# Attention: queries and keys turned by transposing DMA in 16-bit planes instead of on TensorE

## The chip, the cores and the metric

The kernel runs on one core of a Trainium2 chip. The metric is the device time of one execution in microseconds (us), the median of several runs. The engines are called as in the profile: PE is TensorE (PEld its weight loads), DVE is VectorE, ACT is ScalarE, POOL is GpSimd, SP is the engine that issues most transfers. A bank is one of the eight PSUM banks that PE writes, 128 x 512 f32 each.

## The reference

One encoder block over 512 tokens of width 2048, in f32: a combined input projection, two kinds of attention heads, an output projection, and a gated feed-forward block.

```python
h = rmsnorm(x, g_mix[layer])
proj = jnp.einsum('bsd,de->bse', h, w_in[layer])
qa, ka, va, qb, kb, vb = jnp.split(proj, offs, axis=-1)
...
out_a = rmsnorm(mixer_a(qa, ka, va, g_q_a[layer], g_k_a[layer]), g_out_a[layer])
out_b = rmsnorm(mixer_b(qb, kb, vb), g_out_b[layer])
x = x + jnp.einsum('bse,ed->bsd', concat(out_a, out_b), w_out[layer])
h2 = rmsnorm(x, g_ffn[layer])
gate, up = jnp.split(jnp.einsum('bsd,df->bsf', h2, w_gate_up[layer]), 2, axis=-1)
x = x + jnp.einsum('bsf,fd->bsd', jax.nn.silu(gate) * up, w_down[layer])
return rmsnorm(x, g_final)
```

The first kind ("A", `mixer_a`): eight query heads of 128 channels over two key/value heads, RMS-normalised queries and keys with an axial rotary, softmax over all 512 keys. The second kind ("B", `mixer_b`): eight heads with their own keys and values, a rotary on the first 32 channels of each head, and three windowed and dilated branches that are merged by their softmax denominators; the kernel does this as one softmax with an additive mask.

## The kernel before, in words

Every product is made of three matmuls on operands that are split into a high and a low part (`split`: ACT copies the high part, DVE subtracts it from the source for the low part; `mm3`, L228 to L230). The tokens are four row tiles of 128 (`NT`). What PE works on is cut into units: a unit loads a chunk of a weight (`raw`), splits it (`w` or `wide`, `wl`) and multiplies. Program order is written out by hand: each engine runs its instructions in the order in which the Python code issues them, and waits where an operand is not there yet.

Attention has no stage of its own. It is a list of tasks (`attention_tasks`), and `give` hands them out between the matmuls of the projection units: each step of a unit adds credit (`HEAD_RATE`, 2.8 in the first units and 1.3 later), each task costs some. The units beside it are the last chunks of the input projection (`in_plain`; their rows are scaled and evicted by ACT as `evqkB` and stored to DRAM), then chunks of the output projection.

A head is four slots, one for each row tile of its queries. `head_slot(s)` issues what is due in slot s: the score of this slot's head (three matmuls into a bank) and its exponential on ACT, the scaling by the denominator on DVE one slot later, the turn of a block of probabilities on PE five slots later (`pt`, L613, four transposes into one bank, then the split into `pTh` and `pTl`), and the product with the values six slots later (`pv`). Two tasks stand ahead of a head's first score. Four slots ahead, `tq` turns the head's queries: four PE transposes (L563), one for each row tile, into one bank, which is then split into `qTh` and `qTl`. Two slots ahead, `tk` does the same for the keys of a B head (L574); A heads take keys that were turned earlier (`kTA`).

The sources of these turns are `qA[0]` and `qA[1]` (four A heads' queries each, 128 x 512 for a row tile) and `qkB[0]` to `qkB[3]` (two B heads' queries and two B heads' keys each). `qA[1]` and all of `qkB` come back from DRAM by a transfer of 1 MB (`reload`); the rotary of a `qkB` is four DVE operations (`rope_partial`). All these tiles, the planes and words of the change among them, are slots of a shared pool in SBUF that are handed out in turn (`slot`).

The gate and up stage, which follows much later, has a pattern of the same kind: ACT copies a 128 x 512 f32 tile into two planes of 16 bits (L1255), SP issues a transposing transfer of eight 128 x 128 tiles of 16 bits (L1258), and ACT interleaves the planes again (L1264).

Of the kernel before, what the change touches and what calls it, by code (L numbers as in the profile page):

```python
# [14 lines left out]
U16 = mybir.dt.uint16  # L15
AF = mybir.ActivationFunctionType
# [4 lines left out]
P = 128  # L21
S = 512
D = 2048
HD = 128
NT = S // P
# [41 lines left out]
COLUMN_BLOCKS = 3  # L67
SUM_LEAD = 6
ATTEND_PAST = 4


def f32(ap):
# [4 lines left out]
def encoder_block(ctx, tc, x, w_in, g_q_a, g_k_a, w_out, w_gate_up, w_down, g_final, x_t, gains, c_ident, c_mask,  # L77
                  c_axial, c_partial, out):
    nc = tc.nc
# [13 lines left out]
    def slot(base, dtype=F32, shape=(P, 512)):  # L93
        return sp.tile(list(shape), dtype, tag="s", name=nm(base))
# [11 lines left out]
    def bank():  # L106
        return banks.popleft()

    def release(*tiles):
        banks.extend(tiles)  # L110
# [102 lines left out]
    def split(src, name, gain=None, at=None):  # L213
        if at is None:
            hi, lo = slot(name + "h", F32R), slot(name + "l", F32R)
        else:
            hi, lo = (place(*h) for h in at)
        if gain is None:
            nc.scalar.activation(hi, src, AF.Copy)  # L219
            nc.vector.tensor_tensor(lo, src, f32(hi), op=OP.subtract)  # L220
        else:
            nc.scalar.activation(hi, src, AF.Copy, scale=gain)
            nc.vector.scalar_tensor_tensor(lo, src, gain, f32(hi), op0=OP.mult, op1=OP.subtract)
        return hi, lo
# [307 lines left out]
    def rope_partial(q):  # L532
# [7 lines left out]
        nc.vector.tensor_tensor(rot, rot, ropeb[:, 0][:, :, None, :].to_broadcast([P, NT, 4, PARTIAL]), op=OP.mult)  # L540
        nc.vector.tensor_tensor(rot, rot, tmp, op=OP.add)

    oT = {}
    o_dram = {(g, h): dp.tile([P, 512], F32, tag=f"o{g}{h}", name=f"o{g}{h}")
              for g, n in SPILLED.items() for h in range(n)}
# [4 lines left out]
    class Head:  # L550
        def __init__(self, kind, h):
            self.kind, self.h = kind, h
            self.p, self.o = {}, None
            self.negm, self.z, self.rz = None, None, None

        def tq(self):
            ps = bank()
            for t in range(NT):
                if self.kind == "A":
                    src = qA[self.h // 4][t][:, (self.h % 4) * HD:(self.h % 4 + 1) * HD]  # L560
                else:
                    src = qkB[self.h // 2][t][:, (self.h % 2) * HD:(self.h % 2 + 1) * HD]
                nc.tensor.transpose(ps[:, t * P:(t + 1) * P], src, ident)  # L563
            self.q = split(ps, "qT", HD ** -0.5 if self.kind == "B" else None, at=self.home("q"))
            release(ps)

        def tk(self):
            if self.kind == "A":
                self.k = kTA[self.h // (NHA // NKV)]
                return  # L570
            ps = bank()
            for t in range(NT):
                lo = 256 + (self.h % 2) * HD
                nc.tensor.transpose(ps[:, t * P:(t + 1) * P], qkB[self.h // 2][t][:, lo:lo + HD], ident)  # L574
            self.k = split(ps, "kT", at=self.home("k"))
            release(ps)

        def home(self, part):
            return HEAD_HOMES[part][self.h % 2] if self.kind == "B" and self.h > 1 else None
# [79 lines left out]
    def head_slot(s):  # L659
        def at(lag, f, only=None):  # L660
            head, i = head_at(s - lag)
            if head and (only is None or i == only):
                f(head, i)
        at(VALUE_LAG + 1, lambda head, i: head.add_squares(), NT - 1)
        at(0, Head.score)
        at(1, Head.norm)
        at(TURN_LAG, Head.pt)
        at(0, Head.exp)
        at(VALUE_LAG, Head.pv)
        at(VALUE_LAG, lambda head, i: head.fin(), NT - 1)  # L670
        at(-4, lambda head, i: head.tq(), 0)
        at(-2, lambda head, i: head.tk(), 0)

    def weighed(cost, f):
        f.cost = cost
# [2 lines left out]
    def light(cost, tasks):  # L678
        return [weighed(cost, f) for f in tasks]

    def attention_tasks():
        def q_tasks(j):
            return norm_rope(lambda t: (qA[j][t], qA[j][t]), 4, "q")

        def both(cost, *lists):
            return [weighed(cost, lambda fs=fs: [f() for f in fs]) for fs in zip(*lists)]

        qA.update({j: {} for j in range(2)})
        qkB.update({j: {} for j in range(4)})
# [8 lines left out]
        todo += light(0.6, [lambda kv=kv: transpose_k_a(kv) for kv in range(NKV)]) + [heads[0].tq, heads[0].tk]  # L698
        todo += light(0.1, [lambda: reload("qA1", qA[1])])
        extra = {}  # L700

        def at(slot, tasks):
            extra.setdefault(slot, []).extend(tasks)
        at(20, light(0.1, [lambda: nc.sync.dma_start(mask, c_mask)]))
        q_squares, q_turned, q_scaled = q_tasks(1)
        for t in range(NT):
            at(t // 2, both(0.8, q_squares[t:t + 1]))
            at(2 + 2 * t, both(0.9, q_turned[t:t + 1]))
            at(3 + 2 * t, both(0.9, q_scaled[t:t + 1]))
        for j in range(4):  # L710
            s = NT * (NHA + 2 * j)
            at(s - 11, light(0.1, [lambda j=j: reload(f"qkB{j}", qkB[j])]))
            at(s - 7, light(0.9, [lambda j=j: rope_partial(qkB[j]["whole"])]))
        for h in range(NHB):
            s = NT * (NHA + h)
            at(s + 2, light(0.1, [lambda h=h: load_vB(h)]))
            at(s + 4, light(0.4, [lambda h=h: split_vB(h)]))
        for s in range(2 * NHA * NT + VALUE_LAG + 2):
            cost = 1.5 if s < NHA * NT else 1.2 if s < 2 * NHA * NT else 0.7
            todo += [weighed(cost, lambda s=s: head_slot(s))] + extra.get(s, [])  # L720
        return todo
# [122 lines left out]
    class Half(Unit):  # L844
# [784 lines left out]
```

## Time and profile before

| | |
|---|---|
| median of 3 runs | 1951.2 us (1951.03 to 1951.61) |
| profiled run | 1951.23 us, its span 1949.4 us |
| granted clock of PE | 0.999 |
| PE, DVE, ACT, POOL busy in the span | 99%, 79%, 58%, 7% |
| attention, first to last turn of probabilities (L613) | 333.5 to 595.0 us |
| turns of queries on PE (L563, `qA`) | 312.3 to 404.7 us |

The span is the profiled time from the first to the last instruction; the run's own time is 1.8 us longer. A busy share says how much of the span an engine has an instruction in it. A row of a group of instructions gives line, engine, operation, out<-in with the tiles' names, partitions x elements, the count, then the busy time in us and the mean of one in ns, then the idle time of the engine just before them and what ended it. In a timeline the columns are start, length (us), engine, line, operation. Matmuls are pipelined, so a length is longer than the distance between two starts.

### The profile page before, as it was taken

What the parts mean: (1) busy time and instruction counts of PE and PEld (TensorE: products, weight loads), DVE (VectorE), ACT (ScalarE), POOL (GpSimd) and SP (SyncE); (2) the same over time, 40 slices, a digit from 0 to 9 for tenths busy, and PEclk for the clock granted to TensorE, in tenths of its full rate; (3) what the DMA queues carried; (4) which work ended last, traced back from release to release, by engine and by line L of the source; (5) the groups of instructions that cost most, each with busy time, mean ns of one, the idle gap of its engine ahead of it and who ended that gap; (6) DMA issues with size and microseconds to landing.
All of it is one profiled execution on the core that took longest, in us unless ns stands there. A gap on an engine that the chain in (4) does not pass through costs nothing.

```text
span 1949.4 us, 24583 instructions
## 1 busy us (share of the span) xinstructions
PE 1937.3 (99%) x8743; PEld 1599.7 (82%) x8743; DVE 1536.5 (79%) x2012; ACT 1123.3 (58%) x1643; POOL 140.1 (7%) x184
## 2 busy tenths in 40 slices
PE   9999999999999999999999999999999999999998
PEld 7888888888888888888888888888888888888886
DVE  7987768888775697778778777787788978787887
ACT  7755554565455565555555555565555666565555
POOL 1000011000000000000000000000000121111121
PEclk9999999999999999999999999999999999999999
DMA  9677693144342557758767768678587799868865
GB/s 347 233 263 231 212 284 111 59 152 146 103 147 97 184 182 218 268 149 283 233 185 273 224 204 286 183 243 292 141 285 268 212 242 272 229 162 245 235 144 172
DMA packets 252028, 409.30 MB, mean 210 GB/s; under 512 B 58688, under 2 KB 85824, under 8 KB 251776
## 3 DMA queue, kind: packets, MB, share of 16 engines
q1 hardware_dynamic: 221072, 321.12, 50.6%
q0 software_dynamic: 22480, 60.57, 12.4%
q10 hardware_dynamic: 8352, 26.05, 4.1%
q8 instruction: 68, 1.11, 0.2%
q14 instruction: 56, 0.46, 0.1%
HBM read 334.52 MB, written 62.65 MB: 204 GB/s over the span
## 4 chain that ended last, share of the span: by engine, by line
PE 96%; DVE 3%; issue 1%; ACT 0%; DMA 0%; DVEq 0%; POOLq 0%; POOL 0%; SPq 0%; ACTq 0%
PE b L228 31%; PE b L230 31%; PE b L229 31%; PE b L613 1%; PE b L1171 0%; PE b L563 0%; DVE x L1125 0%; DVE w L306 0%; DVE ra L460 0%; DVE tw L896 0%; DVE qA L463 0%; PE b L790 0%; DMA stage<-in_w_in_dram 0%; PE b L574 0%; DVE qA L469 0%
## 5 line engine op out<-in xcount | busy, mean ns | idle before, releaser
L837 ACT ACTIVATE wide<-raw 128x1024 fp32r<-128x1024 f32 x462 | 487.1, 1058 | 455.3 <-PE b L230 265.4
L228 PE MATMUL b<-wide,arena 128*128 128x512 f32 x1848 | 719.6, 389 | 0.0
L840 DVE TENSOR_TENSOR wide<-raw,wide 128x1024 fp32r<-128x1024 f32 x462 | 561.7, 1221 | 200.4 <-ACT wide L837 192.8
L229 PE MATMUL b<-wide,arena 128*128 128x512 f32 x1848 | 719.0, 389 | 0.0
L230 PE MATMUL b<-wide,arena 128*128 128x512 f32 x1848 | 719.0, 389 | 0.0
L229 PEld LDWEIGHTS b<-wide,arena 128*128 128x128 f32 x1848 | 347.0, 188 | 72.1 <-DVE wide L840 0.3
L230 PEld LDWEIGHTS b<-wide,arena 128*128 128x128 f32 x1848 | 347.0, 188 | 71.9
L228 PEld LDWEIGHTS b<-wide,arena 128*128 128x128 f32 x1848 | 347.0, 188 | 71.6
L973 DVE TENSOR_TENSOR raw<-raw,raw 128x1024 f32<-128x1024 f32 x264 | 320.8, 1217 | 10.1 <-DMA raw<-in_w_gate_up_dram 10.1
L229 PE MATMUL b<-tw,arena 128*128 128x512 f32 x396 | 154.3, 390 | 0.6 <-DVE tw L896 0.6
L230 PE MATMUL b<-tw,arena 128*128 128x512 f32 x396 | 154.3, 390 | 0.0
L228 PE MATMUL b<-tw,arena 128*128 128x512 f32 x396 | 154.1, 389 | 0.0
L893 ACT ACTIVATE tw<-stage 128x512 fp32r<-128x512 f32 x140 | 85.4, 628 | 69.4 <-DVE stage L973 43.9
L896 DVE TENSOR_TENSOR tw<-stage,tw 128x512 fp32r<-128x512 f32 x140 | 93.5, 685 | 22.0 <-ACT tw L893 21.9
L228 PE MATMUL b<-w,arena 128*128 128x512 f32 x240 | 95.8, 399 | 0.0
L219 ACT ACTIVATE pTh<-b 128x512 fp32r<-128x512 f32 x64 | 38.2, 597 | 99.8 <-PE b L613 98.1
L230 PE MATMUL b<-w,arena 128*128 128x512 f32 x240 | 93.9, 391 | 0.0
L229 PE MATMUL b<-w,arena 128*128 128x512 f32 x240 | 93.5, 390 | 0.0
L229 PEld LDWEIGHTS b<-tw,arena 128*128 128x128 f32 x396 | 74.3, 188 | 16.7 <-DVE tw L896 1.4
L230 PEld LDWEIGHTS b<-tw,arena 128*128 128x128 f32 x396 | 74.3, 188 | 16.0 <-DVE arena L347 0.3
L228 PEld LDWEIGHTS b<-tw,arena 128*128 128x128 f32 x396 | 74.3, 188 | 15.4
L379 DVE TENSOR_TENSOR pair<-pair 128x256 f32<-128x256 f32 x120 | 46.4, 421 | 46.8 <-ACT pair L1174 23.2
(234 smaller groups left out, 2096.1 us busy)
## 6 DMA issues: line engine op xcount, KB each, us to landing
raw<-in_w_gate_up_dram SPq DMA_DIRECT2D x308, 512.0 KB, 6.3
raw<-in_w_down_dram SPq DMA_DIRECT2D x88, 512.0 KB, 7.7
stage<-in_w_in_dram SPq DMA_DIRECT2D x111, 256.0 KB, 5.3
forms<-pair POOLq DMA_DIRECT2D x22, 896.0 KB, 6.5
fr<-forms ACTq DMA_DIRECT2D x35, 512.0 KB, 6.2
raw<-in_w_out_dram SPq DMA_DIRECT2D x32, 512.0 KB, 4.1
x1d<-s POOLq DMA_DIRECT2D x54, 256.0 KB, 6.8
stage<-in_w_in_dram SPq DMA_DIRECT2D x90, 128.0 KB, 3.5
```

The costliest lines, as they stand in the source:

```text
L219: nc.scalar.activation(hi, src, AF.Copy)
L228: nc.tensor.matmul(dst, ah, bh, start=start, stop=False, skip_group_check=chained)
L229: nc.tensor.matmul(dst, ah, bl, start=False, stop=False, skip_group_check=chained)
L230: nc.tensor.matmul(dst, al, bh, start=False, stop=stop, skip_group_check=chained)
L379: nc.vector.tensor_tensor(out, x, y, op=op)
L613: nc.tensor.transpose(ps[:, t * P:(t + 1) * P], self.p[t][:, kb * P:(kb + 1) * P], ident)
L837: nc.scalar.activation(self.hi, self.src, AF.Copy)
L840: nc.vector.tensor_tensor(self.lo, self.src, f32(self.hi), op=OP.subtract)
L893: nc.scalar.activation(self.pair[:, 0], self.src, AF.Copy)
L896: nc.vector.tensor_tensor(self.pair[:, 1], self.src, f32(self.pair[:, 0]), op=OP.subtract)
L973: nc.vector.tensor_tensor(t[dst], t[src[0]], t[src[1]], op=OP.add if form == "m6" else OP.subtract)
```

## The change

The queries of A heads 2 to 7 and the queries and keys of all B heads are no longer turned on PE. A class `Turned` holds one 128 x 512 x 4 tile. `part(t)`: ACT copies row tile t as 16-bit halves, the two halves of a word in planes apart (128 x 1024, `plane`). `turn(t)`: SP issues a transposing DMA from the plane into `words`. `merge(h)`: ACT interleaves the halves of one head into a 128 x 512 f32 tile in SBUF (`merged`). The split then reads `merged` in place of a bank. A heads 0 and 1 keep `tq`.

```diff
+TURNED_ON_PE = 2
...
+    class Turned:
+        def __init__(self, whole):
+            self.whole, self.planes, self.words = whole, {}, None
+
+        def part(self, t):
+            p = self.planes[t] = slot("plane", U16, (P, 1024))
+            src = self.whole()[:, t].bitcast(U16).rearrange("p (h c s) -> p h s c", h=4, s=2)
+            nc.scalar.activation(p.rearrange("p (h s c) -> p h s c", h=4, s=2), src, AF.Copy)
+
+        def turn(self, t):
+            if self.words is None:
+                self.words = slot("words", U16, (P, NT, 8, P))
+            nc.sync.dma_start_transpose(self.words[:, t], self.planes.pop(t))
+
+        def merge(self, h):
+            m = slot("merged")
+            src = self.words[:, :, 2 * h:2 * h + 2].rearrange("p t s c -> p t c s")
+            nc.scalar.activation(m.bitcast(U16).rearrange("p (t c s) -> p t c s", c=P, s=2), src, AF.Copy)
+            return m
+
+    turned_a = [Turned(lambda j=j: qA[j]["whole"]) for j in range(2)]
+    turned_b = [Turned(lambda j=j: qkB[j]["whole"]) for j in range(4)]
...
+        def by_dma(self):
+            return self.kind == "B" or self.h >= TURNED_ON_PE
...
-        def tk(self):
+        def merge_q(self):
             if self.kind == "A":
+                self.qm = turned_a[self.h // 4].merge(self.h % 4)
+            else:
+                self.qm = turned_b[self.h // 2].merge(self.h % 2)
+
+        def merge_k(self):
+            if self.kind == "B":
+                self.km = turned_b[self.h // 2].merge(2 + self.h % 2)
+
+        def split_q(self):
+            self.q = split(self.qm, "qT", HD ** -0.5 if self.kind == "B" else None, at=self.home("q"))
+
+        def split_k(self):
+            if self.kind == "A":
                 self.k = kTA[self.h // (NHA // NKV)]
-                return
-            ps = bank()
-            for t in range(NT):
-                lo = 256 + (self.h % 2) * HD
-                nc.tensor.transpose(ps[:, t * P:(t + 1) * P], qkB[self.h // 2][t][:, lo:lo + HD], ident)
-            self.k = split(ps, "kT", at=self.home("k"))
-            release(ps)
+            else:
+                self.k = split(self.km, "kT", at=self.home("k"))
...
-        at(-4, lambda head, i: head.tq(), 0)
-        at(-2, lambda head, i: head.tk(), 0)
+
+        def begin(lag, kind, f, dma=True):
+            at(lag, lambda head, i: f(head) if head.kind == kind and head.by_dma() == dma else None, 0)
+        begin(-4, "A", Head.tq, False)
+        begin(-2, "A", Head.split_k, False)
+        begin(-2, "A", Head.split_q)
+        begin(-2, "A", Head.split_k)
+        begin(-3, "A", Head.merge_q)
+        begin(-3, "B", Head.split_q)
+        begin(-4, "B", Head.merge_q)
+        begin(-2, "B", Head.split_k)
+        begin(-3, "B", Head.merge_k)
...
+        def turn_at(turned, slots):
+            for t, s in enumerate(slots):
+                at(s, light(0.05, [lambda t=t: turned.part(t)]))
+                at(s + 1, light(0.05, [lambda t=t: turned.turn(t)]))
+        turn_at(turned_a[0], (0, 1, 2, 2))
+        turn_at(turned_a[1], range(4, 12, 2))
         for j in range(4):
             s = NT * (NHA + 2 * j)
-            at(s - 11, light(0.1, [lambda j=j: reload(f"qkB{j}", qkB[j])]))
-            at(s - 7, light(0.9, [lambda j=j: rope_partial(qkB[j]["whole"])]))
+            at(s - 15, light(0.1, [lambda j=j: reload(f"qkB{j}", qkB[j])]))
+            at(s - 11, light(0.9, [lambda j=j: rope_partial(qkB[j]["whole"])]))
+            turn_at(turned_b[j], range(s - 10, s - 6))
```

In these lists a name with a number is one buffer; `b_72` is a bank, `arena` a region that holds split operands. The line numbers after the change are one higher than before up to the class, and 32 to 49 higher behind it.

ACT, where the first B heads begin, before: the split of the turned keys and the queries of the next head stand among those of the probabilities.

```order
L219 ACTIVATE pTh_3739<-b_77 128x512
L600 ACTIVATE p_3731,fixed<-b_73,fixed 128x512
L219 ACTIVATE kTh_3751<-b_72 128x512
L301 ACTIVATE arena_84<-raw_3391 128x512
L219 ACTIVATE pTh_3777<-b_73 128x512
L600 ACTIVATE p_3769,fixed<-b_77,fixed 128x512
L219 ACTIVATE pTh_3802<-b_73 128x512
L603 ACTIVATE p_3794,fixed<-p_3794,fixed 128x512
L222 ACTIVATE qTh_3814<-b_77 128x512
```

ACT at the same place after the change.

```order
L561 ACTIVATE merged_3752<-words_3527 128x1024
L302 ACTIVATE arena_84<-raw_3383 128x512
L220 ACTIVATE pTh_3781<-b_76 128x512
L632 ACTIVATE p_3773,fixed<-b_71,fixed 128x512
L220 ACTIVATE kTh_3789<-merged_3752 128x512
L551 ACTIVATE plane_3793<-qkB_247_3599 128x1024
L302 ACTIVATE arena_84<-raw_3383 128x512
L223 ACTIVATE arena_85<-oT_3590,fixed 128x512
L220 ACTIVATE pTh_3822<-b_76 128x512
L632 ACTIVATE p_3814,fixed<-b_72,fixed 128x512
L551 ACTIVATE plane_3832<-qkB_247_3599 128x1024
```

A merge and two planes of the next pair (L561, L551) now stand ahead of splits of probabilities (L220), and the split of the keys reads `merged`.

PE at that place before: the turn of the keys, two products of a unit, a score, and the turn of the probabilities.

```order
L574 MATMUL b_72<-fixed,qkB_205_3433 128x128 x4
L228 MATMUL b_76<-arena_84,arena_85 128x512
L229 MATMUL b_76<-arena_84,arena_85 128x512
L230 MATMUL b_76<-arena_84,arena_85 128x512
L228 MATMUL b_75<-arena_84,arena_85 128x512
L229 MATMUL b_75<-arena_84,arena_85 128x512
L230 MATMUL b_75<-arena_84,arena_85 128x512
L228 MATMUL b_77<-arena_85,qTh_3528 128x512
L229 MATMUL b_77<-arena_85,qTh_3528 128x512
L230 MATMUL b_77<-arena_85,qTl_3529 128x512
L613 MATMUL b_73<-fixed,p_3508 128x128
L613 MATMUL b_73<-fixed,p_3541 128x128
```

PE after the change, from a turn of probabilities to the next.

```order
L645 MATMUL b_76<-fixed,p_3540 128x128
L645 MATMUL b_76<-fixed,p_3574 128x128
L645 MATMUL b_76<-fixed,p_3617 128x128
L645 MATMUL b_76<-fixed,p_3667 128x128
L229 MATMUL b_73<-pTh_3781,arena_85 128x512
L230 MATMUL b_73<-pTl_3782,arena_85 128x512
L231 MATMUL b_73<-pTh_3781,arena_85 128x512
L229 MATMUL b_71<-kTh_3789,qTh_3748 128x512
L230 MATMUL b_71<-kTl_3790,qTh_3748 128x512
L231 MATMUL b_71<-kTh_3789,qTl_3749 128x512
L645 MATMUL b_76<-fixed,p_3540 128x128
L645 MATMUL b_76<-fixed,p_3574 128x128
```

The turn of the keys is gone. At this one place the next turn follows into the same bank (`b_76`) with six matmuls of attention between them and none of a unit.

SP before, from the reload of the first pair to that of the second (only the start and the end of the stretch).

```order
L499 DMA qkB_205_3433<-qkB_104 128x4x512
L1097 DMA oback_3435<-oA_108 128x512
L273 DMA raw_3492<-in_w_out_dram 128x2x512
L1097 DMA oback_3494<-oA_109 128x512
L1097 DMA oback_3561<-oA_110 128x512
L273 DMA raw_3609<-in_w_out_dram 128x2x512
```

SP after the change.

```order
L1146 DMA oback_3497<-oA_109 128x512
L556 DMA_TRANSPOSE words_3527<-plane_3493 128x8x128
L556 DMA_TRANSPOSE words_3527<-plane_3529 128x8x128
L1146 DMA oback_3559<-oA_110 128x512
L556 DMA_TRANSPOSE words_3527<-plane_3557 128x8x128
L500 DMA qkB_247_3599<-qkB_105 128x4x512
L274 DMA raw_3637<-in_w_out_dram 128x2x512
L1146 DMA oback_3639<-oA_111 128x512
L556 DMA_TRANSPOSE words_3527<-plane_3597 128x8x128
```

The four turns of the first pair stand among the read-backs of outputs (`oback`), a weight load and the reload of the second pair, which is ahead of the first pair's last turn.

More of the change, by code (lines that the diff above doesn't have):

```diff
@@ L558, in tq @@
             for t in range(NT):
[L559 to L562, printed above, removed]
+                src = qA[self.h // 4][t][:, (self.h % 4) * HD:(self.h % 4 + 1) * HD]
                 nc.tensor.transpose(ps[:, t * P:(t + 1) * P], src, ident)
-            self.q = split(ps, "qT", HD ** -0.5 if self.kind == "B" else None, at=self.home("q"))
+            self.q = split(ps, "qT")
             release(ps)
-        def tk(self):
+        def merge_q(self):
[9 more added lines that the diff above has]
+        def split_k(self):
             if self.kind == "A":
                 self.k = kTA[self.h // (NHA // NKV)]
-                return
-            ps = bank()
-            for t in range(NT):
-                lo = 256 + (self.h % 2) * HD
-                nc.tensor.transpose(ps[:, t * P:(t + 1) * P], qkB[self.h // 2][t][:, lo:lo + HD], ident)
-            self.k = split(ps, "kT", at=self.home("k"))
-            release(ps)
+            else:
+                self.k = split(self.km, "kT", at=self.home("k"))
         def home(self, part):
@@ L697, in attention_tasks @@
         todo += both(2.0, q_squares, k_turned, k_scaled) + both(2.6, q_turned, q_scaled)
-        todo += light(0.6, [lambda kv=kv: transpose_k_a(kv) for kv in range(NKV)]) + [heads[0].tq, heads[0].tk]
+        todo += light(0.6, [lambda kv=kv: transpose_k_a(kv) for kv in range(NKV)]) + [heads[0].tq, heads[0].split_k]
         todo += light(0.1, [lambda: reload("qA1", qA[1])])
```

## The prediction

> **What bounds the kernel now.** I read the page first: its busy shares and its chain.
>
> ```profile
> PE 1937.3 (99%) x8743; PEld 1599.7 (82%) x8743; DVE 1536.5 (79%) x2012; ACT 1123.3 (58%) x1643; POOL 140.1 (7%) x184
> ...
> PE 96%; DVE 3%; issue 1%; ACT 0%; DMA 0%; DVEq 0%; POOLq 0%; POOL 0%; SPq 0%; ACTq 0%
> ```
>
> PE is busy for 99% of the span and the chain that ended last runs through it for 96%. ACT's 58% is an average over the program and says nothing yet of attention. The next view is the waits of PE in the stretch that holds attention, 300 to 620 us.
>
> ```profile
> PE b L563 <- DVE qA L470: 0.5, 1, 0.5
> PE b L228 <- DVE pTl L220: 0.5, 1, 0.5
> ```
>
> PE waits twice there, 0.5 us each. So time is won only by taking work off PE, and lost wherever ACT, DVE or a transfer becomes later than its few spare microseconds. The third view is the table of stretches: length, then busy time of PE, PEld, DVE, ACT and POOL, then clock, share of DMA, GB/s.
>
> ```profile
> 395.00:435.00 40.00, 40.00 (x207) 33.10 (x206) 33.86 (x69) 28.68 (x61) 2.70 (x5) 1.00 0.55 185
> 435.00:475.00 40.00, 39.86 (x205) 32.77 (x204) 34.86 (x79) 24.34 (x51) 1.63 (x2) 1.00 0.38 119
> 320.00:530.00 210.00, 209.33 (x1054) 172.67 (x1053) 167.02 (x353) 123.14 (x281) 12.09 (x17) 1.00 0.37 122
> ```
>
> Over the long stretch ACT is idle for 210 - 123.1 = 86.9 us. Around 395 to 435, where heads of the second kind begin, it is 72% busy and DVE 85%: this is the narrowest place.
>
> **What is removed.** The groups of instructions give the transposes (columns: busy us, mean ns of one, idle before).
>
> ```profile
> L563 PE MATMUL b<-fixed,qA 128*128 128x128 f32 x32 | 5.0, 274 | 0.5 <-DVE qA L470 0.5
> L563 PE MATMUL b<-fixed,qkB 128*128 128x128 f32 x32 | 4.8, 272 | 0.0
> L574 PE MATMUL b<-fixed,qkB 128*128 128x128 f32 x32 | 4.8, 272 | 0.0
> ```
>
> Heads 0 and 1 keep theirs, so 24 + 32 + 32 = 88 matmuls go, in 22 groups of four. A duration is not a price on a pipelined engine; the timeline of PE around one group is.
>
> ```profile
> 404.10 0.39 PE L230 MATMUL b<-pTh,arena 128*128 128x512 f32 x1
> 404.33 0.60 PE L563 MATMUL b<-fixed,qA 128*128 128x128 f32 x4
> 404.69 0.48 PE L228 MATMUL b<-w,arena 128*128 128x512 f32 x1
> 405.00 0.39 PE L229 MATMUL b<-w,arena 128*128 128x512 f32 x1
> 405.23 0.40 PE L230 MATMUL b<-w,arena 128*128 128x512 f32 x1
> ```
>
> Two 512-wide matmuls normally start 0.23 us apart (404.10 to 404.33). Without the group L228 would start at 404.33 and L229 at 404.56; it starts at 405.00. A group costs 0.44 us, the same that the chain of waits books for it:
>
> ```profile
> 363.36 0.44 PE b L563 x4
> ...
> 547.83 0.44 PE b L563 x4
> ```
>
> These two are the first and the last of seven such pieces. So 22 x 0.44 = **9.7 us** leave PE. If the second of the two waits goes with its cause, 0.5 more; it stands at the start of the first head's values, where the order changes, and I count it gone (0 to 0.5).
>
> [...]
>
> **What is added on ACT.** 24 copies into planes and 22 merges. The same two operations stand in the gate and up stage, in the same shapes.
>
> ```profile
> L1255 ACT ACTIVATE pair<-s 128x1024 uint16<-128x1024 uint16 x40 | 40.7, 1041 | 0.0
> ...
> L1264 ACT ACTIVATE pair<-turned 128x1024 uint16<-128x1024 uint16 x20 | 23.3, 1167 | 2.9 <-DMA forms<-pair 2.9
> ...
> L219 ACT ACTIVATE qTh<-b 128x512 fp32r<-128x512 f32 x8 | 4.8, 595 | 2.0 <-PE b L563 2.0
> ...
> L219 ACT ACTIVATE arena<-vraw 128x512 fp32r<-128x512 f32 x6 | 3.8, 627 | 0.0
> ```
>
> 24 x 1.04 + 22 x 1.17 = 50.7 us. The splits now read SBUF instead of a bank: 22 x (0.627 - 0.595) = 0.7 us. That 51 us is under the 86.9 us idle, and most of it lies beside PE at no cost; what isn't covered is local. In the order of ACT, the part of the program that stood at 395 to 435 gets eight planes (of the first two pairs) and six merges: 8 x 1.04 + 6 x 1.17 = 15.3 us, less 0.1 each because neighbours on ACT overlap by that (325.35 + 1.26 against 326.49 in the rows further down), 13.9. ACT needs 28.7 + 13.9 = 42.6 us, PE now 40 - 4 x 0.44 = 38.2. ACT falls 4.4 us behind. How much of that PE feels depends on the slack of a step of attention:
>
> ```profile
> 396.79 0.60 PE L613 MATMUL b<-fixed,p 128*128 128x128 f32 x4
> ...
> 400.00 0.60 PE L613 MATMUL b<-fixed,p 128*128 128x128 f32 x4
> 400.36 0.48 PE L228 MATMUL b<-pTh,arena 128*128 128x512 f32 x1
> 400.67 0.39 PE L229 MATMUL b<-pTl,arena 128*128 128x512 f32 x1
> ```
> ```profile
> 397.43 0.60 ACT L219 ACTIVATE pTh<-b 128x512 fp32r<-128x512 f32 x1 [0.44 <-PE b L613]
> ```
> ```profile
> 398.30 0.69 DVE L220 TENSOR_TENSOR pTl<-b,pTh 128x512 fp32r<-128x512 f32 x1
> ```
>
> A turn of p starts at 396.79, and ACT and DVE have split it at 398.99, 2.2 us later; its bank is wanted at 400.00 and its low half at 400.67. The slack is 1.0 to 1.7; I take 1.2, and 4.4 - 1.2 = **3.2 us** of stall. Ends: 0, if the queue ahead of ACT lets all its 11.3 idle us be used earlier, and 8, if the copies wait at the wrong moments and DVE (85%) can't catch up either. From 435 on ACT has 24.3 + some 11 us of work in 38: it recovers, and I charge nothing.
>
> **Two smaller places on ACT.** Two planes of the first query tile stand ahead of the evictions of a projection unit:
>
> ```profile
> 325.35 1.26 ACT L490 ACTIVATE evqkB<-b,fixed 128x512 f32<-128x512 f32 x2
> 326.49 0.69 ACT L600 ACTIVATE p<-b,fixed 128x512 f32<-128x512 f32 x1
> ...
> 327.69 1.26 ACT L490 ACTIVATE evqkB<-b,fixed 128x512 f32<-128x512 f32 x2
> ```
>
> ACT works without a gap there, so 2 x 0.95 = 1.9 us are added before banks come free that PE wants. I take **1.0** (0 to 1.9). At the end of attention the last two steps follow each other with no unit between them: three scores are gone too, and PE has 1.4 us (six matmuls at 0.23) where the split above needs 2.2: **0.7** (0 to 0.9).
>
> **What is added on SP.** 24 transposing transfers, and four reloads of qkB four slots earlier. The gate and up stage has the same transfer 40 times; its row gives the time on SP, then the landing.
>
> ```profile
> L1258 SPq DMA_TRANSPOSE turned<-pair x40: 1231/1534/3287, 763.6 to 1455.6; - x40
> ...
> DMA to landing us min/median/max: 3.1/4.8/7.6
> ```
>
> The merge of a head follows the last turn of its four by two slots, 2 x 3.2 = 6.4 us at 395 to 435 (396.79 to 400.00 is one). Issue and landing take 1.5 + 4.8 = 6.3 us at the median: just hidden. At the longest landing, 9.1: 2.7 late, less the 1.2 of slack. This is tight at four sets (both tiles of the first kind, the first two pairs of the second); in later slots the gap is wider:
>
> ```profile
> 447.03 0.44 PE b L563 x4
> 467.11 0.44 PE b L563 x4
> ```
>
> Four slots take 20.1 us there, two 10. I take **0.3 us** in all (0 to 6). The reload moves from 11 slots ahead to 15, with rope on DVE after four slots, 12.8 us, against its landing:
>
> ```profile
> qkB<-qkB SPq DMA_DIRECT2D x4, 1024.0 KB, 6.9
> ```
>
> Hidden. Behind a turn on SP stand weight loads, which are issued several units ahead; 1.5 us more per transfer I cost at nothing, covered by that lead. On DVE nothing is added; rope only moves.
>
> [...]
>
> **Sum.** The profiled run took 1951.23 us, 1.8 of it around the span, and stands on the median of 1951.2. -9.7 - 0.5 + 3.2 + 1.0 + 0.7 + 0.3 = -5.0: **1946.2 us**.
>
> **Rivals.** *All of the copies are covered.* ACT's idle time is usable and the slack of several banks takes the rest: only the 0.7 at the end stays, 1951.2 - 9.7 = 1941.5. For it speak the 11.3 us idle in the narrow stretch; against it that ACT would need 42.6 us in 38.2.
>
> *ACT and DVE eat the gain.* The stall at 395 to 435 is 6 to 8 us, since ACT's copies delay the exponentials and splits that DVE, 85% busy, waits for, and the three smaller terms are 2 to 3: 9.7 + 0.5 comes back, 1950.5.
>
> *Slower: merges wait for the planes.* ACT works in order. A merge whose words have not landed holds up every split and exponential behind it, and PE one step later. If at the four tight sets landing is L, each costs 1.5 + L - 6.4 - 1.2. With the other terms at my values (4.9), slower by over 0.2%, 3.9 us, needs 10.2 + 3.9 - 4.9 = 9.2 us from the four, 2.3 each: L = 8.4, above the longest of 40 by 0.8. At L = 10 it would be 3.9 each: 1951.2 - 10.2 + 4.9 + 15.6 = 1961.5; at 9, 1957.5. What speaks for it is that two of these turns stand behind a reload of 1 MB and weights on SP; against it the row of landings.
>
> [...]
>
> **Chances.** Forecast 0.42 (own range 1943.5 to 1949), all covered 0.24, gain eaten 0.22, slower 0.12. 0.2% is 3.9 us, about what a measurement of this kernel can tell from no change, so faster ends at 1947.3. Two thirds of my own case lie under it: 0.28 + 0.24 = 0.52. The rest of it and the eaten gain, 0.14 + 0.22, are 0.36; slower is 0.12. The range runs from 1941.0, the full gain, to 1952.5, the eaten gain with a late landing or two; it leaves out the slower case and little else.
>
> **What would show it.** PE's matmuls must fall from 8743 by 88. In PE's waits new entries must name the turn of p or the values after ACT's pTh, with 2 to 5 us in the heads around the first pair of the second kind, and an entry on the projection's banks near 327. ACT's planes and merges must be near 1.04 and 1.17 us, the landings near 4.8 us, and ACT's idle time ahead of the merges must name the transfer only rarely. If ACT has no backlog, the stall term is wrong and the time is nearer 1941.5; if its idle time names the words in several merges, the landing term is. I would be wrong altogether if PE waits on a weight load: transfers that hold up SP.

## The result, and the profile after

The changed kernel is slower: 1963.1 us (median of 4 runs, 1961.9 to 1964.5) against 1951.4, a ratio of 1.0058 (95% interval 1.0041 to 1.0075), some 11 us. The profiled run took 1961.88 us, its span 1960.1: 10.7 more than before. In this part a ratio stands for the measured time over that of the kernel before on the same chip, and a thousandth of it is 1.95 us.

The page after, busy shares and chain:

```profile
PE 1935.1 (99%) x8655; PEld 1594.0 (81%) x8655; DVE 1536.6 (78%) x2012; ACT 1168.7 (60%) x1689; POOL 140.2 (7%) x184
...
PE 92%; DVE 4%; ACT 2%; DMA 1%; issue 1%; SPq 0%; DVEq 0%; POOLq 0%; POOL 0%; ACTq 0%
```

The 88 matmuls are gone (8743 to 8655), ACT has 46 instructions more. But the chain now leaves PE for 8% of the span instead of 4%. The waits of PE from 300 to 640 us, where there were two of 0.5 us:

```profile
PE b L645 <- DVE pTl L221: 6.7, 4, 3.2
PE b L229 <- ACT arena L223: 2.9, 1, 2.9
PE b L645 <- DVE fixed L625: 2.1, 1, 2.1
PE b L645 <- DVE p L640: 0.7, 1, 0.7
PE b L587 <- DVE qA L471: 0.6, 1, 0.6
PE b L230 <- DVE pTl L221: 0.5, 2, 0.3
```

That is 13.5 us against 1.0. All the large ones lie between 417 and 467 us. The same stretch, 400 to 480 us, in the table of stretches, first of the kernel before and then of the changed one (length, busy of PE, PEld, DVE, ACT, POOL, then the clock granted to PE, share of DMA, GB/s):

```profile
400.00:480.00 80.00, 79.86 (x412) 65.95 (x411) 68.94 (x147) 52.08 (x108) 3.80 (x6) 1.00 0.47 153
```
```profile
400.00:480.00 80.00, 68.23 (x305) 53.87 (x304) 57.47 (x121) 58.59 (x107) 3.26 (x5) 0.91 0.49 130
```

PE has 305 records of matmuls where it had 412, and its clock is 0.91. A finer cut shows where the clock falls:

```profile
430.00:435.00 5.00, 1.83 (x9) 1.61 (x10) 4.37 (x9) 3.04 (x6) 0.00 (x0) 0.94 0.00 0
435.00:440.00 5.00, 2.83 (x9) 1.92 (x9) 3.93 (x10) 3.42 (x7) 0.00 (x0) 0.50 0.33 65
440.00:445.00 5.00, 5.00 (x22) 4.04 (x22) 2.30 (x6) 4.04 (x8) 0.00 (x0) 0.88 0.49 93
450.00:455.00 5.00, 3.63 (x11) 2.94 (x12) 4.72 (x13) 2.76 (x7) 0.00 (x0) 0.66 1.11 330
465.00:470.00 5.00, 2.89 (x11) 2.06 (x11) 3.58 (x7) 2.53 (x4) 0.00 (x0) 0.85 0.23 84
470.00:475.00 5.00, 5.00 (x24) 4.22 (x23) 3.91 (x10) 3.40 (x6) 0.58 (x1) 0.81 0.00 0
```

The clock drops at the waits, down to 0.50 from 435 to 440 us. Behind the second of them the wide matmuls start 0.42 us apart instead of 0.23:

```profile
439.31 0.63 PE L230 MATMUL b<-pTl,arena 128*128 128x512 f32 x1
439.73 0.63 PE L231 MATMUL b<-pTh,arena 128*128 128x512 f32 x1
```

The six stretches of 5 us with what they lack of 1.00 come to 5 x (0.06 + 0.50 + 0.12 + 0.34 + 0.15 + 0.19) = 6.8 us, an upper end, since part of it lies in the waits themselves. The account of the span, with the prediction's 9.7 for the transposes: 9.7 off, 13.5 - 1.0 = 12.5 on for waits, up to 6.8 for the clock, at most 9.6 in all; measured 10.7.

### The profile page after: what moved, and what is told of

The parts are those of the page before. It is cut to its first block, busy times and chain, and to the rows that moved or that the text cites. A ratio compares the mean times of both kernels' runs of the same rounds, so it can differ in the third digit from the quotient of the medians.

```text
span 1960.1 us, 24503 instructions
## 1 busy us (share of the span) xinstructions
PE 1935.1 (99%) x8655; PEld 1594.0 (81%) x8655; DVE 1536.6 (78%) x2012; ACT 1168.7 (60%) x1689; POOL 140.2 (7%) x184
## 4 chain that ended last, share of the span: by engine, by line
PE 92%; DVE 4%; ACT 2%; DMA 1%; issue 1%; SPq 0%; DVEq 0%; POOLq 0%; POOL 0%; ACTq 0%
PE b L231 30%; PE b L230 30%; PE b L229 30%; PE b L645 1%; DMA words<-plane 0%; DVE x L1174 0%; PE b L1220 0%; DVE w L307 0%; DMA raw<-in_w_in_dram 0%; DMA stage<-in_w_in_dram 0%; DVE ra L461 0%; DVE fixed L621 0%; DVE tw L945 0%; ACT p L632 0%; DVE qA L464 0%
## 5 line engine op out<-in xcount | busy, mean ns | idle before, releaser
L1324 POOL DMA_DIRECT2D forms<-pair x22 | 20.1, 914 | 777.4 <-DVE pair L380 751.2
```

The source lines that it names most:

```text
L1324: nc.gpsimd.dma_start(forms_dram[:, :, n], hpart[0][:, 256:].rearrange("p (f c) -> p f c", c=256))
```

## Experiments

**The transfers.** The words of the first pair's last turn stand out in the changed kernel: the turn's times on SP, and landings.

```profile
L556 SPq DMA_TRANSPOSE words<-plane x24: 1232/1238/2612, 323.2 to 533.3; - x24
...
DMA to landing us min/median/max: 3.0/3.3/11.2
```

SP just before it, then ACT (start, length), and the times that ACT's queue stood at a semaphore of a merge (min, median, max in ns):

```profile
409.57 0.38 SPq L500 DMA_DIRECT2D qkB<-qkB  x1
410.40 0.38 SPq L274 DMA_DIRECT2D raw<-in_w_out_dram  x1
410.88 0.42 SPq L1146 DMA_DIRECT2D oback<-oA  x1
411.39 2.61 SPq L556 DMA_TRANSPOSE words<-plane  x1
```
```profile
422.77 1.18 ACT L561 ACTIVATE merged<-words 128x1024 uint16<-128x1024 uint16 x1 [1.90 <-issue]
```
```profile
L561 ACTq EVENT_SEMAPHORE  x8: 17/28/3338, 337.9 to 541.2; - x8
```

This turn was issued behind 1 MB of reload, 512 KB of weights and 256 KB of outputs, landed 11.2 us later (411.39 + 11.2 = 422.6), and the merge held ACT for 1.9 us. The profile names no releaser for that wait; its end at the landing and the one long stand at a semaphore speak for the words. The first theory was that this starts everything. First run, the reload moved behind the turn:

```diff
-            at(s - 15, light(0.1, [lambda j=j: reload(f"qkB{j}", qkB[j])]))
+            at(s - 14, light(0.1, [lambda j=j: reload(f"qkB{j}", qkB[j])]))
```

> The changed kernel with the reload of each qkB issued one slot later, so that it stands behind the last turn of the pair before on SP instead of ahead of it. Theory 'late words': the 11.2 us landing of the first pair's last turn, behind 1 MB of reload and 0.5 MB of weights, starts the waits of PE at 417 to 475 us and the lowered clock there; the turn now lands in 3 to 5 us, the 1.9 us wait ahead of the merge goes, and the time falls to 1943 to 1952. Theory 'ACT load': the 51 us of copies are too much for ACT around 400 to 475 whenever the words come; the time stays at 1958 to 1964.

Ratio 1.0042 (1.0029 to 1.0054), 1959.9 us. The landings are as hoped:

```profile
DMA to landing us min/median/max: 3.0/3.1/5.7
```

The time is what "ACT load" expected: 3 us are won back, 8 stay. In this run the weights and the read-back stand behind the turn in SP's order as well, so it takes all of the 1.75 MB from ahead of the turn, not the reload alone. The next run takes the transfers away altogether:

```diff
-            p = self.planes[t] = slot("plane", U16, (P, 1024))
+            if self.words is None:
+                self.words = slot("words", U16, (P, NT, 8, P))
+            p = self.words[:, t].rearrange("p a c -> p (a c)")
...
-            nc.sync.dma_start_transpose(self.words[:, t], self.planes.pop(t))
+            pass
```

> The changed kernel without the 24 transposing transfers: ACT writes the planes where the words would land, and the merges read them there, so the queries and keys are not turned; all planes, merges and splits stay. 'Late words': no merge can wait for a transfer, time 1942 to 1950. 'ACT load': the same copies, the same backlog, 1956 to 1963.

Ratio 1.0039 (1.0025 to 1.0052), 1958.2 us. Its waits of PE in 415 to 480 us:

```profile
PE b L645 <- DVE pTl L221: 3.7, 3, 2.0
PE b L229 <- ACT arena L223: 3.0, 1, 3.0
PE b L645 <- DVE fixed L625: 2.1, 1, 2.1
```

They are those of the first run within 0.2 us, and the clock in this stretch is 0.92. "Late words" carries 0.0019 of the loss, 3.7 us, and no more. (The intervals of the two ratios overlap; the times do not, 1961.9 to 1964.5 with the transfers and 1958.0 to 1961.4 without.) Whether that turn was late for its place behind the reload in SP's queue or for the bytes ahead of it, the next one asks:

```diff
-        nc.sync.dma_start(whole, spill[name].rearrange("t p c -> p t c"))
+        (nc.gpsimd if name.startswith("qkB") else nc.sync).dma_start(whole, ...)
```

> The changed kernel with the four reloads of qkB issued by POOL instead of SP; orders on PE and ACT are the same. If the last turn was late because it stood behind the reload in SP's queue, it lands in 4 to 6 us and the time falls to 1944 to 1953. If it was late because the reload, the weights and the stores of the projection share the transfer engines with it, it still lands after 8 to 11 us and the time stays at 1957 to 1964.

Ratio 1.0059 (1.0046 to 1.0071), and the longest landing is longer still:

```profile
DMA to landing us min/median/max: 3.0/3.2/13.0
```

It is the same turn, and with the reload on another queue it is as late. So its place behind the reload in SP's queue is not the reason, and the bytes in flight are what is left; the weights and one read-back still stood ahead of it on SP, and how the transfers share the engines was not tried apart.

**The floor: no turns at all.** The kernel before with the transposes left out, `tk` likewise:

```diff
         def tq(self):
+            if self.kind == "B" or self.h >= 2:
+                src = (qA[self.h // 4] if self.kind == "A" else qkB[self.h // 2])[self.h % 4]
+                self.q = split(src, "qT", HD ** -0.5 if self.kind == "B" else None, at=self.home("q"))
+                return
...
-            self.k = split(ps, "kT", at=self.home("k"))
-            release(ps)
+            self.k = split(qkB[self.h // 2][self.h % 4], "kT", at=self.home("k"))
```

> The kernel before without the 88 transposes on PE: the splits of these heads read a row tile in SBUF as it is, so the queries and keys are not turned; nothing is added on ACT, DVE or SP. It measures the term of PE alone. Priced by the distance of starts, 22 x 0.44 = 9.7 us: 1941 to 1942.5. If the groups lay beside other work, less: 1945 to 1951. If the whole durations count (88 x 0.272 = 23.9 us): 1927.

Ratio 0.9962 (0.9949 to 0.9974): 7.4 us less than before, 5.1 to 10. The price by the distance of starts holds within that, and the whole durations don't. Its waits give back 1.1 of the 2.3 us that are missing from 9.7: the 0.5 at the first head's values has grown to 1.0, and two of 0.3 are new.

```profile
PE b L228 <- DVE pTl L220: 1.0, 1, 1.0
PE b L229 <- DVE pTl L220: 0.6, 2, 0.3
```

**The order alone.** The changed kernel with planes, transfers and merges left out; reloads, rotaries, lags and credits stay.

```diff
         def part(self, t):
-            ...
+            pass
         def turn(self, t):
-            ...
+            pass
         def merge(self, h):
-            ...
+            return self.whole()[:, h]
```

> The changed kernel without planes, transfers and merges: its order of tasks, reloads and rotaries is kept, and the splits read a row tile of the source as it is (the queries and keys are not turned). Theory 'copies': the 46 copies on ACT make the waits at 417 to 475 us; without them the time is that of the kernel without the PE turns, 1943 to 1946. Theory 'order': two slots of attention that now follow each other with only six matmuls between two turns of p, and the rotary that DVE does just ahead of them, make the waits and the lowered clock by themselves; the time is 1950 to 1957.

Ratio 0.9993 (0.9984 to 1.0002). Without one copy or transfer, 0.0031 of the gain is gone: 6.0 us. The rest of the way to the run without transfers, 0.0046 or 9.0 us, is the copies' in this order. DVE of this kernel, where PE waits for it:

```profile
422.31 0.68 DVE L221 TENSOR_TENSOR pTl<-b,pTh 128x512 fp32r<-128x512 f32 x1
...
424.33 0.69 DVE L224 SCALAR_TENSOR_TENSOR qTl<-qkB,qTh 128x512 fp32r<-128x512 f32 x1 [1.35 <-ACT qTh L223]
424.94 0.75 DVE L538 TENSOR_TENSOR rotary<-qkB,rotary 128x256 f32<-128x256 f32 x2
425.73 0.69 DVE L541 TENSOR_TENSOR qkB<-qkB,rotary 128x512 f32<-128x512 f32 x1
426.46 0.69 DVE L542 TENSOR_TENSOR qkB<-qkB,rotary 128x512 f32<-128x512 f32 x1
427.07 0.68 DVE L307 TENSOR_TENSOR arena<-raw,arena 128x512 fp32r<-128x512 f32 x1
427.67 0.74 DVE L1147 SCALAR_TENSOR_TENSOR arena<-oback,fixed,arena 128x512 fp32r<-128x512 f32 x1
428.33 0.68 DVE L667 TENSOR_TENSOR acc<-acc,sq 128x512 f32<-128x512 f32 x1
428.93 0.68 DVE L614 TENSOR_REDUCE fixed<-b 128x1 f32<-128x512 f32 x1
...
430.12 0.68 DVE L221 TENSOR_TENSOR pTl<-b,pTh 128x512 fp32r<-128x512 f32 x1
```
```profile
430.87 0.66 PE L638 MATMUL b<-fixed,p 128*128 128x128 f32 x4 [2.03 <-DVE pTl L221]
```

DVE stands idle for 1.35 us in front of the queries' low part, whose high part ACT now makes behind the two copies that end a head; then it works through the moved rotary and six more instructions, and the low part of p, for which PE waits, comes last at 430.12, 7.8 us after the one before it. The rotary is that of the second pair. In the kernel before it started at 437.7 us, between two low parts of p that were only 4.5 us apart (437.05 and 441.57), and PE had no wait behind it.

This also says where the copies cost their 9.0 us. Not at the first wait: the run without transfers, which has all copies, waits 2.05 us there (430.7) and the order alone 2.03, and just ahead of it ACT is idle for DVE. The copies bring two waits further on:

```profile
429.52 0.69 ACT L632 ACTIVATE p<-b,fixed 128x512 f32<-128x512 f32 x1 [3.28 <-DVE fixed L621]
```
```profile
447.46 0.93 PE L645 MATMUL b<-fixed,p 128*128 128x128 f32 x4 [2.12 <-DVE fixed L625]
463.30 0.50 PE L229 MATMUL b<-arena,arena 128*128 128x512 f32 x1 [2.96 <-ACT arena L223]
```

From 300 to 640 us all listed waits of PE come to 10.6 us in that run and to 7.2 in the order alone, 3.4 apart. The other part is the clock: 0.87 from 430 to 470 us, which is up to 40 x 0.13 = 5.2 us, against 1.00 in the order alone. A third of that (1.7 us, 430 to 435) stands behind the first wait, which is no longer than in the order alone; why the clock fell there and not here is open.

**Short gaps, as the whole cause.** In the order of PE the changed kernel has two places with only six wide matmuls between two turns of p (before there were at least 12 in the body of attention). One number spreads them again:

```diff
-            at(s - 15, light(0.1, [lambda j=j: reload(f"qkB{j}", qkB[j])]))
-            at(s - 11, light(0.9, [lambda j=j: rope_partial(qkB[j]["whole"])]))
+            at(s - 14, light(0.1, [lambda j=j: reload(f"qkB{j}", qkB[j])]))
+            at(s - 11, light(0.6, [lambda j=j: rope_partial(qkB[j]["whole"])]))
```

> The changed kernel with the reload behind the last turn, as in the first experiment, and one more number: the rotary of qkB costs 0.6 credits instead of 0.9. In the order on PE, no two turns of p have fewer than 12 wide matmuls between them in the body of attention any more (the changed kernel has two places with six). All copies and transfers stay. 'Order': the waits at these places go, PE's clock stays up, 1944 to 1951. 'Copies': ACT has the same 51 us to do in the same stretch, 1956 to 1960, as without this edit.

Ratio 1.0043 (1.0030 to 1.0056), the same as with the gaps. So with the copies in, spreading the gaps wins nothing. The wait stays where it was (431.5 us, 430.8 in the first run), and is longer:

```profile
PE b L645 <- DVE pTl L221: 3.7, 1, 3.7
```

**The rotary, cut into row tiles.** In the order alone, and with all copies:

```diff
-            at(s - 11, light(0.9, [lambda j=j: rope_partial(qkB[j]["whole"])]))
+            for t in range(NT):
+                at(s - 11 + t, light(0.2, [lambda j=j, t=t: rope_partial(qkB[j]["whole"], slice(t, t + 1))]))
```

> The order-alone kernel (no planes, transfers or merges; the splits read a row tile as it is) with the rotary of each qkB cut into its four row tiles, one a slot from 11 slots ahead on, 0.2 credits each in place of 0.9 at once. Theory 'rotary in the narrow part': of the 6 us that the order alone costs, most comes from the second pair's rotary, four DVE operations in a row that moved from slot 33 to slot 29, where slots are 12 matmuls long and DVE has no room; cut up, the wait of 2.0 us at 431 and the one behind it shrink below 1, and the time is 1945 to 1948. Rival 'short gap': the place with six matmuls between two turns makes the waits; it is still there once, and the time stays at 1949 to 1952.

> The changed kernel with the reload behind the last turn (first experiment) and the rotary cut into four. 'Rotary in the narrow part' with the copies on top: 4 to 6 us less than the first experiment's 1959.9, so 1954 to 1956. If the copies on ACT alone carry the waits there, no change, 1958 to 1961. If rotary and copies only hurt together, 1946 to 1950.

Ratios 1.0012 (1.0003 to 1.0021) and 1.0075 (1.0063 to 1.0088): both worse than with the rotary whole, by 0.0019 and 0.0033, against every expectation. The rows of two of its lines, cut (order alone) and whole (changed kernel):

```profile
L538 DVE TENSOR_TENSOR rotary<-qkB,rotary 128x64 f32<-128x64 f32 x32 | 5.6, 218 | 0.0
L542 DVE TENSOR_TENSOR qkB<-qkB,rotary 128x128 f32<-128x128 f32 x16 | 4.7, 292 | 0.5
```
```profile
L538 DVE TENSOR_TENSOR rotary<-qkB,rotary 128x256 f32<-128x256 f32 x8 | 3.0, 418 | 0.0
L542 DVE TENSOR_TENSOR qkB<-qkB,rotary 128x512 f32<-128x512 f32 x4 | 2.8, 693 | 0.1
```

A quarter of the elements takes some half of the time (218 ns against 418, 292 against 693). With the third line, L541, which has the same busy times as the second, that is 15.0 us instead of 8.6 on the engine that was short. The cut spread the load and raised it, so it says nothing on the place.

**Which part of the order.** Two runs on the order alone, one thing each: the rotary and reload back where they were, and the queries' split one slot earlier.

```diff
-            at(s - 15, light(0.1, [lambda j=j: reload(f"qkB{j}", qkB[j])]))
-            at(s - 11, light(0.9, [lambda j=j: rope_partial(qkB[j]["whole"])]))
+            at(s - 11, light(0.1, [lambda j=j: reload(f"qkB{j}", qkB[j])]))
+            at(s - 7, light(0.9, [lambda j=j: rope_partial(qkB[j]["whole"])]))
```

> The order-alone kernel (no planes, transfers or merges) with reload and whole rotary back where they were before, 11 and 7 slots ahead; the split of the queries stays at 3 slots ahead for the second kind. Theory 'moved rotary': the 2.2 us of DVE that now fall between A's last slots are most of the 6 us (7.6 of the two comparisons) that the order alone costs; time 1944 to 1947. Theory 'moved split': DVE waits 1.35 us with an empty queue behind it for the queries' high part, which ACT now does after the two copies that end a head; then the time stays at 1949 to 1951.

```diff
-        begin(-3, "B", Head.split_q)
-        begin(-4, "B", Head.merge_q)
+        begin(-4, "B", Head.split_q)
+        begin(-5, "B", Head.merge_q)
```

> The order-alone kernel with the split of the queries of the second kind at 4 slots ahead, as before the change, instead of 3; reload and rotary stay early, and the order on PE is the same, instruction for instruction. 'Moved split': the 1.35 us idle of DVE ahead of that split goes, the wait of 2.0 us at 431 shrinks under 1, and the time is 1946 to 1949. 'Moved rotary': 1950 to 1952.

Ratios 0.9972 (0.9961 to 0.9983) and 0.9981 (0.9973 to 0.9990), against 0.9993. Putting the rotary and its reload back is worth 0.0021, 4.1 us; the intervals just do not overlap. Moving the split is worth 0.0012, 2.3 us, and there the intervals overlap. Together that is 6.4 us, about the 6; no run has both.

Two things stay open. Putting the rotary back also takes one of the two gaps of six matmuls off PE, the one at 434.8, so rotary and gap are not told apart. In the order alone the wait of 2.03 us stands behind a gap of 18 matmuls, the one of 1.92 behind this gap of six, and the other gap of six, at 451.8, has no wait; so a short gap alone makes none. And with the split moved the first wait is gone, but the second is 2.20 and the clock behind it 0.86 and 0.79 (430 to 435 and 435 to 440 us), where the order alone kept 1.00.

**The copies: amount or place.** The whole change, with the chain of the first two pairs moved to where A's slots still have room, the queries' split one slot earlier as above, and its own order alone (which again leaves the queries and keys unturned):

```diff
-            at(s - 15, light(0.1, [lambda j=j: reload(f"qkB{j}", qkB[j])]))
-            at(s - 11, light(0.9, [lambda j=j: rope_partial(qkB[j]["whole"])]))
-            turn_at(turned_b[j], range(s - 10, s - 6))
+            r = (12, 18, 33, 41)[j]
+            at(r, light(0.1, [lambda j=j: reload(f"qkB{j}", qkB[j])]))
+            at(r + 3, light(0.9, [lambda j=j: rope_partial(qkB[j]["whole"])]))
+            turn_at(turned_b[j], range(r + 4, r + 8))
```

> The whole change, with the chain of reload, rotary, planes and turns of the first two pairs moved out of the stretch where slots are 12 matmuls long and A's outputs are split (reload at slots 12 and 18 instead of 17 and 25, of the last two pairs at 33 and 41 as before it, rotary 3 slots later, planes from 4 slots later on), and the split of B's queries at 4 slots ahead, as it was before the change. All copies and transfers stay. Theory 'place': copies, rotary and transfers cost only where they stand in the narrow stretch; time 1944 to 1950. Theory 'amount': 51 us of copies on ACT cost some 9 us wherever they stand; 1953 to 1960.

> The order of the run before this one without planes, transfers and merges (the splits read a row tile as it is). 'Place' and 'amount' agree on 1943.5 to 1948 for this one; what they differ on is the distance from it to the run with copies: 0 to 3 us by 'place', 8 to 12 us by 'amount' (it was 9 us in the order of the change).

Ratios 0.9990 (0.9981 to 0.9999) and 0.9970 (0.9959 to 0.9981). The same 24 planes, 22 merges and 24 transfers cost 0.0020, 3.9 us, over their order here, and 0.0065, 12.7 us, in the change. It is their place far more than their amount, though 3.9 is a little above what "place" allowed, and known to some 3 us only: the runs of this order alone spread from 1944.4 to 1949.9. The largest waits of the early chain are small, and its clock is 1.00 from 395 to 520 us, so no clock term comes on top:

```profile
PE b L645 <- DVE pTl L221: 1.5, 5, 0.4
PE b L229 <- DVE pTl L221: 1.1, 2, 0.5
```

**A version that beats both.** The first two pairs stay on PE as before; A heads 2 to 7 and the last two pairs go by transfer, with the reload of these pairs one slot later, as in the first experiment.

```diff
+PAIRS_ON_PE = 2
-            return self.kind == "B" or self.h >= TURNED_ON_PE
+            return self.h >= (PAIRS_ON_PE * 2 if self.kind == "B" else TURNED_ON_PE)
...
+            late = 4 if j < PAIRS_ON_PE else 0
+            at(s - 15 + late + (not late), light(0.1, [lambda j=j: reload(f"qkB{j}", qkB[j])]))
+            at(s - 11 + late, light(0.9, [lambda j=j: rope_partial(qkB[j]["whole"])]))
+            if not late:
+                turn_at(turned_b[j], range(s - 10, s - 6))
```

> The changed kernel with the first two of the four pairs of the second kind turned on PE as before, with their reload and rotary 11 and 7 slots ahead; A heads 2 to 7 and the last two pairs stay with the transfers. 14 of the 22 groups are gone from PE, at 7.7/22 = 0.35 us each (the measured gain without any turns) 4.9 us. 'Copies': the narrow stretch at 400 to 475 has no planes of these pairs and 8 merges fewer, so 1946 to 1948. 'Order': one place with six matmuls between two turns is left, 1948 to 1953.

Ratio 0.9981 (0.9972 to 0.9990), 3.7 us faster than before. This does not decide between the two expectations: the ratio makes 1947.5 of the 1951.2, in the range of 'Copies', and the median of its own runs is 1948.8, in that of 'Order'. With the rotary of the last two pairs cut into four:

> The kernel with the first two pairs on PE and the rest by transfer, with the rotary of the last two pairs cut into four. There the waits were 1.3 us and 0.6 us at 502 us behind a whole rotary and a residual addition on DVE. 'Rotary': both shrink, 1 to 2 us less than the 1948.8 without the cut: 1946 to 1948. 'Copies': no change.

Ratio 0.9976 (0.9966 to 0.9985), 1948.1 us: the fastest kernel here that does the whole computation, some 4.7 us under the one before. Whether the cut helped in this place is open, since the two intervals overlap. Its two largest waits are 0.7 and 0.6 us.

## Why the prediction was wrong

The sum said -5.0, 1946.2 us, faster; measured is +11. By its steps:

- *PE, -9.7.* Right in kind and within the interval of the run that measures it (-7.4, 5.1 to 10).
- *The wait that was to go, -0.5.* It went, and one of 0.7 on p (L640) stands at 334.6 us in its place.
- *"On DVE nothing is added; rope only moves", 0.* The step that failed first. 6.0 us come from the order alone, and 4.1 come back when the rotary and its reload return to their old slots. I had the row with DVE 85% busy in front of me and asked only whether the reload would land in time, not what stands behind four DVE operations in a row at the new place.
- *Copies, 3.2 + 1.0 + 0.7.* The second step that failed: measured 9.0 in this order. The durations were right:

```profile
L561 ACT ACTIVATE merged<-words 128x1024 uint16<-128x1024 uint16 x22 | 26.0, 1184 | 2.0 <-issue 1.9
...
L551 ACT ACTIVATE plane<-qkB 128x1024 uint16<-128x1024 uint16 x16 | 16.8, 1050 | 0.0
```

  The place and the price were not. At 395 to 435, where ACT was to fall 4.4 us behind, the copies add nothing to the wait (2.05 us against 2.03 without them), and ACT itself waits 3.28 us for DVE. "From 435 on it recovers, and I charge nothing" is where they cost: waits of 2.1 and 3.0 us at 447 and 463 in the run without transfers, 451 and 467 in the changed kernel, and the lowered clock with them. The two smaller terms were not there: no wait at 327, and 0.2 us at the end of attention.
- *The clock, not in the sum.* A wait was priced at its own length. Up to 6.8 us of lowered clock followed, more than any term for waiting that I had set down; these microseconds are part of the 9.0 and 3.7 here, not added to them.
- *Transfers, 0.3.* Measured 3.7. The bound of 7.6 us for a landing came from another stage, where no more than one weight load of 512 KB stands directly ahead of a turn on SP, not 1.75 MB. Of 24 landings one exceeded it, at 11.2. The sum "1.5 + 4.8" also counts the 1.5 us on SP twice, since a landing is counted from the start of the issue (411.39 + 11.2 is where the merge starts); that made the turns look tighter than they were. I had seen in the order that the reload stands ahead of that turn and named it only in a rival.
- *The rivals.* "Slower" needed all four tight sets late by 2.3 us each; one was late, and the kernel without transfers is slow as well. Nearest is "ACT and DVE eat the gain": that the low part of p comes late from a busy DVE held, but the first such wait is the order's and not the copies', and the size of 6 to 8 us did not hold, because it knew nothing of the rotary and the clock.

Turning on PE stayed the faster way against this change as it stands (1.0058). The transfers themselves do not decide that: they landed in 3.3 us at the median, they carry 3.7 of the 11 us, and the whole change in other slots is no slower than PE (0.9990).

## What to carry to other kernels

When work is moved off a bound engine, cost what moves along with it at its new place: the instructions on the other engines that now stand, in program order, ahead of what the bound engine waits for, and the largest transfers issued just before the new ones. Read the busy shares of all engines in the stretch where it lands, not in the stage as a whole, and try the order without the work and the work without the order; here the order cost 6 us and the copies 9, and moving the same copies and transfers by some slots took their loss from 12.7 to 3.9. Where PE may be held up as here, add a term for its clock: one wait of 2.05 us was followed by 0.66 over 5 us, one of 2.03 by 1.00, and in the copies' 9 the term was up to 5.2.

## What the runs showed of the hardware

PE's clock fell to 0.50 in the changed kernel (435 to 440 us), behind a wait of 3.18 us ahead of 433.2; I had priced a wait at its own length alone. In the kernel without transfers a single wait of 2.05 us ahead of 430.7 is followed by a stretch at 0.66 (430 to 435 us). In the order alone a wait of 2.03 us at 430.9 and another of 1.9 behind it left the clock at 1.00, and in the run with the rotary put back one of 2.2 did too (1.00 in every stretch of 5 us from 425 to 475). The wait and the stretch of the first, then the stretch of the second:

```profile
430.73 1.12 PE L645 MATMUL b<-fixed,p 128*128 128x128 f32 x4 [2.05 <-DVE pTl L221]
```
```profile
430.00:435.00 5.00, 3.57 (x10) 2.57 (x10) 4.00 (x9) 4.06 (x10) 0.00 (x0) 0.66 0.00 0
```
```profile
430.00:435.00 5.00, 2.21 (x12) 1.61 (x13) 4.74 (x10) 3.39 (x8) 0.00 (x0) 1.00 0.01 2
```

So the length alone does not decide; what else does, no run shows. A drop lasts the same each time here, or twice that. In stretches of 1 us the changed kernel has the clock at 0.73, 0.50, 0.50 and 0.56 from 451 to 455 us, and at 0.77, 0.50, 0.50 and 0.53 from 468 to 472. What they lack of 1.00 is 1.7 us each, at 0.50 an estimated 1.7/0.50 = 3.4 us of lowered clock. By the same estimate 0.66 over 5 us in the kernel without transfers is 5 x 0.34/0.50 = 3.4 us, and so are 0.66 at 450 and 0.85 + 0.81 at 465 to 475 us in the changed kernel; its 0.94 + 0.50 + 0.88 at 430 to 445 are twice that, 6.8 us.

A transposing transfer of eight tiles, which landed in 3.0 us at the least and 3.3 at the median, took 11.2 behind 1.75 MB of other transfers that were issued in the 2 us before it, and 13.0 with 1 MB of them issued by POOL.
